# A diffusion trunk on one core: the experts' scatter through a sum of its own, and a finer spread of the modulation sums

## Chip, cores and metric

One core of one Trainium2 chip runs the whole kernel. The metric is the device time of one execution in microseconds, the median of several runs.

## What is computed

Two layers over 256 latent and 256 context tokens of width 1024, all in float32. Each layer modulates its input by vectors that come from a conditioning vector, mixes tokens (a recurrence, windowed attention, differential attention, one projection in and one out), adds and normalises; then a channel mixer, again modulated, gated and normalised. The channel mixer of layer 0 is a dense SwiGLU, that of layer 1 a top-2-of-8 mixture of SwiGLU experts over the latent tokens alone:

```
mod = split(silu(c) @ ada_w[layer] + ada_b[layer], 6)
u = h * (1 + mod[4]) + mod[3]
layer 0: f = (silu(u @ w1) * (u @ w3)) @ w2
layer 1: f = sum over e of combine[:, e] * swiglu(u, w1[e], w3[e], w2[e])
h = layer_norm(alpha * h + mod[5] * f, ln_g, ln_b)
```

The product with `mod[5]` is the same for all experts of a token row, column by column.

## The kernel before

Every weight is split into a high and a low part (`split`, L117 to L128): ScalarE copies a 128x1024 tile to `whi` (L126), VectorE subtracts it from the raw tile into `wlo` (L127), and TensorE makes three products of each pair (L107 to L109). The split tiles come from the pool `wp` with 5 buffers for each of the two parts, for all stages; the split of `w2` in the dense SwiGLU alone has another pool with 4. Raw weights come in tiles of 1 MB, issued in order from the SyncE queue.

**Dense SwiGLU** (`ffn`, L893 to L983). The hidden width of 2816 is worked in 11 steps of 256. `up(s)` loads and splits w1 and w3 of a step (two raw buffers, the pool `rawp`) and makes two parts, f = 0 and 1, of 48 products each, with SiLU and product on ScalarE and VectorE. `down(s)` makes 8 outputs of 6 products each in two PSUM banks (`ps_T`); VectorE copies (L956, step 0) or adds (L958) each into `acc`. The order is up(0); then for s = 0 to 8: up(s + 1), `fill(s)`, down(s); then up(10) and `last`. `fill` runs up to 4 pieces of another list, the modulation sums of layer 1 (`ada_vector`, L302 to L338). A piece loads 1 MB of `ada_w` into one of the same two raw buffers, and VectorE multiplies and adds it into `acca` (L319, L321): four operations where the vector is wanted for both kinds of tokens (vectors 0 and 1), two otherwise (vectors 2 to 5). After four such pieces the end of a vector transposes and reduces (L331, L332) and adds a bias (L337). There are 33 pieces in all, and one wait hangs on the first: `acca` lies where the layer norm's gains (`lg`, `lb`) lay, which GpSimd reads in `base` (L890).

**Mixture of experts** (`moe`, L1226 to L1309). Tokens are gathered into units of 128 for one expert; 7 units run, written out one behind another, and a loop for further ones runs no time with these inputs. A unit takes 33 raw tiles of 1 MB. `wtile` (L1066 to L1075) gives each a buffer in turn: 7 of the pool `rawb`, then 2 of `rawp`, so 9 tiles can be on the way or wait. `up` and `down` split and multiply them. At the end of a unit `scatter` (L1185 to L1200) splits its output Y, multiplies it with a selection matrix (two 128-row blocks by two halves of 512 columns, PSUM bank `ps_T`), and for each of the four results VectorE multiplies by the router's weight and by the gate row `mod[5]` into `sct` (L1199, two buffers), and GpSimd adds `sct` into the stream `hl` (L1200). In the last unit VectorE takes half of the adds.

The instructions of an engine stand in an order that is fixed when the program is built: a scheduler interleaves the parts by its own estimates, in the order of the source where it can. Each engine then works in that order.

Of the kernel before, what the change touches and what calls it, by code (L numbers as in the profile page):

```python
# [15 lines left out]
F32 = mybir.dt.float32  # L16
# [4 lines left out]
ALU = mybir.AluOpType  # L21
# [3 lines left out]
P = 128  # L25
D = 1024
KD = D // P
T = 512
# [8 lines left out]
UNITS = 7  # L37
# [39 lines left out]
class Trunk:  # L77
# [41 lines left out]
    def split(self, v, pool=None):  # L119

        nc = self.nc
        a, b = v.shape[1], v.shape[2]
        pool = pool or self.wp
# [260 lines left out]
    def fill(self, n):  # L384

        for _ in range(min(n, len(self.todo))):
            self.todo.pop(0)()
# [505 lines left out]
    def ffn(self, uh, ul, h, pools, gate, fill):  # L893
        nc, i = self.nc, self.i
        accp, raw2, wp2, gp = pools
# [6 lines left out]
        def up(s):  # L902
# [18 lines left out]
            for f in range(2):  # L921
                if s:
# [24 lines left out]
        def down(s, gs, gate):  # L947
            fs = [*zip(gs, w2_parts(s))]
            for tb in range(NTB):
                for n in range(2):  # L950
# [21 lines left out]
        for s in range(NS - 2):  # L972
            if s == NS - 4:
                with self.tc.issue_after(self.last.ins):
                    gate = gate()
            nxt = up(s + 1)
            fill(s)
            down(s, gs, gate)
            gs = nxt
        fs = [*zip(gs, w2_parts(NS - 2))]  # L980
        gs = up(NS - 1)
        fill(NS - 2)
# [202 lines left out]
    def scatter(self, Y, selT, cu, gate, hl, quick=False):  # L1185
# [6 lines left out]
        for b in range(2):  # L1192
            for nn in range(2):
                cs = slice(nn * 512, nn * 512 + 512)
                o = self.bank("h" if quick else "T")
                nc.tensor.matmul(o, lhsT=selT[:, b], rhs=yh[:, cs], start=True, stop=False)
                nc.tensor.matmul(o, lhsT=selT[:, b], rhs=yl[:, cs], start=False, stop=True)
                t = mp.tile([P, 512], F32, name="sct", tag="g" if quick and nn else "sct")
                nc.vector.scalar_tensor_tensor(out=t, in0=o, scalar=cu[:, b:b + 1], in1=gate[:, cs], op0=ALU.mult, op1=ALU.mult)  # L1199
                (nc.vector if quick and nn else nc.gpsimd).tensor_tensor(out=hl[:, b, cs], in0=hl[:, b, cs], in1=t, op=ALU.add)  # L1200
# [27 lines left out]
    def moe(self, hl, u, gate, ro, rs, pool, first):  # L1228
# [4 lines left out]
        gb = self.gains(1, 0, xr)  # L1233
        u32 = rp.tile([P, KD, 2 * P], F32, name="u32r")
# [34 lines left out]
        Y = None  # L1269
        for u in range(UNITS):  # L1270
# [20 lines left out]
            self.scatter(Y, selT, cu[:, :, u], gate, hl, u == UNITS - 1)  # L1291
# [3 lines left out]
        with tc.For_i(UNITS, n, 1) as u:  # L1295
# [12 lines left out]
            self.scatter(Y, selT, pc[:, 1], gate, hl)  # L1308
        return fin  # L1309

    def run(self):
# [5 lines left out]
        with ExitStack() as es:  # L1317
# [4 lines left out]
            self.wp = pool("wp", 5)  # L1322
# [35 lines left out]
            with tc.tile_pool(name="hc", bufs=1) as hcp:  # L1358
# [9 lines left out]
                with tc.tile_pool(name="acc", bufs=1) as accp, tc.tile_pool(name="raw2", bufs=1) as raw2, tc.tile_pool(name="wp2", bufs=4) as wp2, \  # L1368
# [5 lines left out]
                    with tc.tile_pool(name="ga", bufs=3) as gp:  # L1374
# [5 lines left out]
                        self.ffn(uh, ul, h, (accp, raw2, wp2, fg), lambda: self.gate(0, 5, [0, 1], gp, "x4"), lambda s: self.fill(4))  # L1380
# [23 lines left out]
            self.RB, self.wn = 7, 0  # L1404
            self.rawb = pool("rawb", self.RB)
            ro = pool("ro", 1)
# [56 lines left out]
```

## Time and profile before

| | us |
|---|---|
| runs, median (3 runs) | 1658.87 (1657.64 to 1660.73) |
| profiled execution, its own time | 1661.47 |
| profiled execution, its span | 1659.6 |
| TensorE busy (share of the span) | 1559.6 (94%) |
| VectorE busy | 1305.5 (79%) |
| ScalarE busy | 915.9 (55%) |
| GpSimd busy | 157.7 (10%) |

The rest of a time outside the span is 1.9 us. Times inside the trace count from the start of the span. The dense SwiGLU lies at about 318 to 717, the mixer of layer 1 at 717 to 880, the units of the experts at 929 to 1643. In the rows PE is TensorE, DVE VectorE, ACT ScalarE, POOL GpSimd, SP SyncE, whose queue issues the loads.

### The profile page before, as it was taken

How to read it: one execution, taken by the hardware profiler on the slowest of the kernel's cores; microseconds unless marked ns; L12 is line 12 of the kernel's file. 1: busy time of each engine (PE TensorE's matmuls, PEld its weight loads, DVE VectorE, ACT ScalarE, POOL GpSimd, SP SyncE). 2: the span in 40 equal slices, each digit the busy share in tenths (PEclk: the TensorE clock that was granted, in tenths of full speed). 3: DMA queues.
4: the chain of work that ended last, by engine and by line, in shares of the span. 5: the costliest groups of instructions: out<-in, count | busy, mean ns of one | idle time of the engine just before them, and what ended most of it. 6: DMA issues, size and time to landing. Idle time of an engine off the chain costs nothing. (4 is left out here: it accounts for less than half of the span.)

```text
span 1659.6 us, 21231 instructions
## 1 busy us (share of the span) xinstructions
PE 1559.6 (94%) x7753; PEld 1228.5 (74%) x7753; DVE 1305.5 (79%) x1835; ACT 915.9 (55%) x1292; POOL 157.7 (10%) x132
## 2 busy tenths in 40 slices
PE   7999999996999999989798799999999999999995
PEld 3776566785888887777576588787877878878774
DVE  2678674669977666677976999999888898888987
ACT  2466565422222222246765578777776767767673
POOL 0000011250000000250002200101000010010101
PEclk9999999997999999999799899999999999999998
DMA  9313446335556553112216599898998989989890
GB/s 306 122 57 102 153 153 203 101 129 162 207 188 196 185 183 122 52 60 77 76 26 254 211 394 352 333 360 309 350 353 310 335 322 342 356 306 339 326 351 31
DMA packets 167655, 364.78 MB, mean 220 GB/s; under 512 B 8396, under 2 KB 46120, under 8 KB 165496
## 3 DMA queue, kind: packets, MB, share of 16 engines
q1 hardware_dynamic: 162544, 355.56, 60.9%
q0 software_dynamic: 1840, 6.67, 1.2%
q10 hardware_dynamic: 3160, 1.12, 0.3%
q8 instruction: 64, 1.05, 0.2%
q14 instruction: 47, 0.39, 0.1%
HBM read 362.27 MB, written 1.05 MB: 219 GB/s over the span
## 5 line engine op out<-in xcount | busy, mean ns | idle before, releaser
L127 DVE TENSOR_TENSOR wlo<-rawb,whi 128x1024 fp32r<-128x1024 f32 x362 | 436.1, 1249 | 34.4 <-ACT whi L126 30.7
L126 ACT CAST whi<-rawb 128x1024 fp32r<-128x1024 f32 x362 | 364.3, 1051 | 56.8 <-PE ps_h L109 33.7
L126 ACT CAST whi<-raw 128x1024 fp32r<-128x1024 f32 x214 | 218.7, 1051 | 185.0 <-PE ps_T L109 86.1
L127 DVE TENSOR_TENSOR wlo<-raw,whi 128x1024 fp32r<-128x1024 f32 x214 | 268.7, 1283 | 46.2 <-ACT whi L126 44.7
L108 PE MATMUL ps_h<-wlo,th 128*128 128x512 f32 (+1 forms) x672 | 257.9, 384 | 14.2 <-DVE wlo L127 13.2
L107 PE MATMUL ps_h<-whi,th 128*128 128x512 f32 (+1 forms) x672 | 253.7, 378 | 0.2 <-ACT th L131 0.2
L109 PE MATMUL ps_h<-whi,tl 128*128 128x512 f32 (+1 forms) x672 | 251.7, 375 | 0.0
L108 PEld LDWEIGHTS ps_h<-wlo,th 128*128 128x128 f32 x672 | 127.3, 189 | 51.2 <-DVE wlo L127 30.5
L107 PEld LDWEIGHTS ps_h<-whi,th 128*128 128x128 f32 x672 | 127.2, 189 | 23.2 <-ACT th L131 0.5
L109 PEld LDWEIGHTS ps_h<-whi,tl 128*128 128x128 f32 x672 | 127.5, 190 | 20.7 <-DVE tl L132 0.3
L108 PE MATMUL ps_Y<-wlo,gTh 128*128 128x512 f32 x308 | 122.4, 397 | 0.4
L109 PE MATMUL ps_Y<-whi,gTl 128*128 128x512 f32 x308 | 120.3, 390 | 0.0
L1200 POOL TENSOR_TENSOR hl<-hl,sct 128x512 f32<-128x512 f32 x26 | 45.0, 1760 | 679.2 <-DVE sct L1199 679.2
L107 PE MATMUL ps_Y<-whi,gTh 128*128 128x512 f32 x308 | 108.3, 390 | 0.0
L107 PE MATMUL ps_acc<-uh,whi 128*128 128x512 f32 (+1 forms) x256 | 92.5, 367 | 2.3 <-ACT whi L126 2.3
L108 PE MATMUL ps_acc<-ul,whi 128*128 128x512 f32 (+1 forms) x256 | 94.3, 369 | 0.1
L109 PE MATMUL ps_acc<-uh,wlo 128*128 128x512 f32 (+1 forms) x256 | 92.2, 361 | 0.0
L108 PE MATMUL ps_S<-ul,whi 128*128 128x512 f32 (+1 forms) x240 | 85.6, 357 | 0.0
L107 PE MATMUL ps_S<-uh,whi 128*128 128x512 f32 (+1 forms) x240 | 85.5, 357 | 0.0
L109 PE MATMUL ps_S<-uh,wlo 128*128 128x512 f32 (+1 forms) x240 | 85.0, 355 | 0.0
L107 PE MATMUL ps_T<-whi,gh 128*128 128x512 f32 x152 | 61.5, 404 | 16.8 <-DVE acc L956 14.6
L321 DVE SCALAR_TENSOR_TENSOR acca<-raw,sc,acca 128x1024 f32<-128x1024 f32 x56 | 70.2, 1278 | 5.3 <-DMA raw<-in_ada_w_dram 5.1
(362 smaller groups left out, 2895.2 us busy)
## 6 DMA issues: line engine op xcount, KB each, us to landing
rawb<-in_moe_w_dram SPq DMA_DIRECT2D x181, 1024.0 KB, 6.5
raw<-in_moe_w_dram SPq DMA_DIRECT2D x50, 1024.0 KB, 6.6
raw<-in_ada_w_dram SPq DMA_DIRECT2D x40, 1024.0 KB, 5.1
raw<-in_ffn_w_dram SPq DMA_DIRECT2D x33, 1024.0 KB, 5.3
raw<-in_w_in_dram SPq DMA_DIRECT2D x16, 1024.0 KB, 5.1
aw<-in_ada_w_dram SPq DMA_DIRECT2D x16, 512.0 KB, 6.8
raw<-in_w_out_dram SPq DMA_DIRECT2D x16, 512.0 KB, 5.0
lg<-in_ln_g_dram POOLq DMA_DIRECT2D x4, 512.0 KB, 4.1
```

Of the source, the lines that this page charges most:

```text
L107: mm(out, lhsT=ah, rhs=bh, start=start, stop=False)
L108: mm(out, lhsT=ah, rhs=bl, start=False, stop=False)
L109: mm(out, lhsT=al, rhs=bh, start=False, stop=stop)
L126: nc.scalar.copy(out=hi, in_=v)
L127: self.last = nc.vector.tensor_tensor(out=lo, in0=v, in1=hi, op=ALU.subtract)
L321: STT(out=acc[t], in0=r[:, k - k0], scalar=x, in1=acc[t], op0=ALU.mult, op1=ALU.add)
L1200: (nc.vector if quick and nn else nc.gpsimd).tensor_tensor(out=hl[:, b, cs], in0=hl[:, b, cs], in1=t, op=ALU.add)
```

## The change

- `scatter` hands each of its four results to a function. For units 0 to 5 it is `add_sum`: VectorE multiplies by the router's weight and adds into a sum tile of 128x2048, in one operation (unit 0 multiplies only). GpSimd has no part in it.
- After unit 5 `fold` runs on GpSimd: two products of the sum with the gate row and two adds into `hl`, each 128x1024. Unit 6 goes as before (`add_last`).
- The split tiles of the experts and of what is split just ahead of them take a sixth pair of buffers (`wpx`), in turn with the five. The raw tiles of the experts have 5 buffers in place of 7, so 7 with the two of `rawp`. A small tile `shift` moves the addresses behind it.
- In `ffn` the pieces of the modulation sums no longer stand four together between up(s + 1) and down(s). From s = 1 on one stands ahead of each of the two parts of up(s + 1), and one ahead of the second and the fourth row block of down(s). Step 0 has none. What is left (one piece of 33) runs ahead of `last`.

```
--- before.py
+++ after.py
@@ -120,7 +120,9 @@
 
         nc = self.nc
         a, b = v.shape[1], v.shape[2]
-        pool = pool or self.wp
+        if pool is None:
+            pool = self.wps[self.ws % len(self.wps)]
+            self.ws += 1
         hi = pool.tile([P, 1024], F32R, name="whi", tag="whi")[:, 0:a * b].rearrange("p (a b) -> p a b", a=a)
         lo = pool.tile([P, 1024], F32R, name="wlo", tag="wlo")[:, 0:a * b].rearrange("p (a b) -> p a b", a=a)
         nc.scalar.copy(out=hi, in_=v)
@@ -899,7 +901,7 @@
         acc = accp.tile([P, NTB, D], F32, name="acc")
         NS = FF // 256
 
-        def up(s):
+        def up(s, fill=None):
             ws = []
             for w in (w1, w3):
                 r = self.raw(w[:, :, s * 256:(s + 1) * 256])
@@ -919,6 +921,8 @@
                         for f in range(2):
                             product(bs[f][j], ws[j], f, t0, t1)
             for f in range(2):
+                if fill:
+                    fill(1)
                 if s:
                     b1, b3 = self.bank("acc"), self.bank("S")
                     product(b1, ws[0], f, 0, T)
@@ -944,9 +948,11 @@
             for j, ((gh, gl), (wh, wl)) in enumerate(fs):
                 self.mm3(b, gh[:, t], gl[:, t], wh[:, 0, cs], wl[:, 0, cs], j == 0, j == len(fs) - 1)
 
-        def down(s, gs, gate):
+        def down(s, gs, gate, fill):
             fs = [*zip(gs, w2_parts(s))]
             for tb in range(NTB):
+                if fill and tb % 2:
+                    fill(1)
                 for n in range(2):
                     cs = slice(n * 512, n * 512 + 512)
                     b = self.bank("T")
@@ -973,13 +979,12 @@
             if s == NS - 4:
                 with self.tc.issue_after(self.last.ins):
                     gate = gate()
-            nxt = up(s + 1)
-            fill(s)
-            down(s, gs, gate)
+            nxt = up(s + 1, fill if s else None)
+            down(s, gs, gate, fill if s else None)
             gs = nxt
         fs = [*zip(gs, w2_parts(NS - 2))]
         gs = up(NS - 1)
-        fill(NS - 2)
+        fill(99)
         last(fs + [*zip(gs, w2_parts(NS - 1))], gate)
 
 
@@ -1182,7 +1187,7 @@
             self.split2(th[:, ks], tl[:, ks], pt.rearrange("p (k t) -> p k t", k=4))
         return th, tl
 
-    def scatter(self, Y, selT, cu, gate, hl, quick=False):
+    def scatter(self, Y, selT, cu, add):
 
         nc, mp = self.nc, self.mp
         yh, yl = (mp.tile([P, D], F32R, name=name, tag="rows") for name in ("yh", "yl"))
@@ -1192,12 +1197,39 @@
         for b in range(2):
             for nn in range(2):
                 cs = slice(nn * 512, nn * 512 + 512)
-                o = self.bank("h" if quick else "T")
+                o = self.bank("h" if add is self.add_last else "T")
                 nc.tensor.matmul(o, lhsT=selT[:, b], rhs=yh[:, cs], start=True, stop=False)
                 nc.tensor.matmul(o, lhsT=selT[:, b], rhs=yl[:, cs], start=False, stop=True)
-                t = mp.tile([P, 512], F32, name="sct", tag="g" if quick and nn else "sct")
-                nc.vector.scalar_tensor_tensor(out=t, in0=o, scalar=cu[:, b:b + 1], in1=gate[:, cs], op0=ALU.mult, op1=ALU.mult)
-                (nc.vector if quick and nn else nc.gpsimd).tensor_tensor(out=hl[:, b, cs], in0=hl[:, b, cs], in1=t, op=ALU.add)
+                add(b, nn, o, cu[:, b:b + 1])
+
+    def add_sum(self, b, nn, o, cu):
+
+        S = self.sum[:, b, nn * 512:nn * 512 + 512]
+        if (b, nn) in self.summed:
+            self.nc.vector.scalar_tensor_tensor(out=S, in0=o, scalar=cu, in1=S, op0=ALU.mult, op1=ALU.add)
+        else:
+            self.nc.vector.tensor_scalar(S, o, cu, None, ALU.mult)
+        self.summed.add((b, nn))
+
+    def add_last(self, b, nn, o, cu):
+
+        cs = slice(nn * 512, nn * 512 + 512)
+        t = self.mp.tile([P, 512], F32, name="sct", tag="g" if nn else "sct")
+        self.nc.vector.scalar_tensor_tensor(out=t, in0=o, scalar=cu, in1=self.gate2[:, cs], op0=ALU.mult, op1=ALU.mult)
+        (self.nc.vector if nn else self.nc.gpsimd).tensor_tensor(out=self.hl[:, b, cs], in0=self.hl[:, b, cs], in1=t, op=ALU.add)
+
...
+    def fold(self):
+
+        for op in (ALU.mult, ALU.add):
+            for b in range(2):
+                S = self.sum[:, b]
+                self.nc.gpsimd.tensor_tensor(out=S if op == ALU.mult else self.hl[:, b], in0=S, in1=self.gate2 if op == ALU.mult else self.hl[:, b], op=op)
 
     def moe_consts(self, ro):
 
@@ -1231,6 +1263,8 @@
         xr, rp = pool("xr", 1, "right"), rs.enter_context(tc.tile_pool(name="rq", bufs=1))
         xh, xl = xr.tile([P, 2, D], F32R, name="xh"), xr.tile([P, 2, D], F32R, name="xl")
         gb = self.gains(1, 0, xr)
+        self.sum, self.summed, self.hl, self.gate2 = xr.tile([P, 2, D], F32, name="sum"), set(), hl, gate
+        self.add_last = self.add_last
         u32 = rp.tile([P, KD, 2 * P], F32, name="u32r")
         lt, logit = rp.tile([P, 2, P], F32, name="lt"), ro.tile([P, 2, NE], F32, name="logit")
         lg, lp = self.bank("T"), self.bank("T")
@@ -1288,7 +1322,9 @@
                     Y = [self.bank("Y") for _ in range(2)]
                 self.down(e, c, gt, Y)
                 g = nxt
-            self.scatter(Y, selT, cu[:, :, u], gate, hl, u == UNITS - 1)
+            self.scatter(Y, selT, cu[:, :, u], self.add_last if u == UNITS - 1 else self.add_sum)
+            if u == UNITS - 2:
+                self.fold()
             if u + 1 < UNITS:
                 x, selT = x2, selT2
         n = nc.values_load(nu[0:1, 0:1], min_val=0, max_val=NU)
...
@@ -1319,7 +1355,7 @@
             self.cp = pool("cp", 1)
             self.stp = pool("stp", 4)
             self.rawp = pool("rawp", 2)
-            self.wp = pool("wp", 5)
+            self.wps, self.ws = [pool("wp", 5)] * 5, 0
             pool("edge", 1, side="right").tile([P, 24], F32, name="edge")
             mx = ExitStack()
             right = lambda name, bufs, **kw: mx.enter_context(tc.tile_pool(name=name, bufs=bufs, side="right", **kw))
@@ -1377,7 +1413,7 @@
                         self.todo = sum((self.ada_vector(1, c, [0, 1], gp, rw) for c in range(2)), [])
                         self.todo += [lambda: m1.extend(self.mods(1, 0, (0, 1)))]
                         self.todo += sum((self.ada_vector(1, c, [0], gp, rw) for c in range(2, 6)), [])
-                        self.ffn(uh, ul, h, (accp, raw2, wp2, fg), lambda: self.gate(0, 5, [0, 1], gp, "x4"), lambda s: self.fill(4))
+                        self.ffn(uh, ul, h, (accp, raw2, wp2, fg), lambda: self.gate(0, 5, [0, 1], gp, "x4"), self.fill)
                         self.fill(99)
 
                 self.rest = "res"
@@ -1401,8 +1437,10 @@
             self.moe_consts(pool("rc", 1))
             mh, ml = self.mixer(1, uh, ul, lat, bd, self.lru_products(1, uh, ul, True), prepare)
             self.dumpm(mh, ml, 1)
-            self.RB, self.wn = 7, 0
+            self.RB, self.wn = 5, 0
             self.rawb = pool("rawb", self.RB)
+            pool("shift", 1).tile([P, 32], F32, name="shift")
+            self.wps, self.ws = self.wps + [pool("wpx", 1)], 0
             ro = pool("ro", 1)
             gate2 = self.gate(1, 5, [0], ro)[0]
             with ExitStack() as ms:
```

## Rows read from the trace of the kernel before

**Rows 1.** Busy tenths of TensorE, 40 equal slices of the span.

```profile
PE   7999999996999999989798799999999999999995
```

**Rows 2.** Engines by stretch: busy us (count) per engine, granted clock, DMA share, GB/s.

```profile
360.00:380.00 20.00, 12.51 (x56) 10.02 (x54) 15.36 (x16) 1.12 (x2) 3.93 (x2) 0.89 0.32 106
380.00:400.00 20.00, 12.87 (x45) 10.32 (x46) 17.36 (x22) 5.55 (x7) 0.00 (x0) 0.68 0.57 176
420.00:440.00 20.00, 19.91 (x91) 16.19 (x90) 19.53 (x30) 4.28 (x5) 0.00 (x0) 1.00 0.47 168
...
1240.00:1260.00 20.00, 17.20 (x69) 13.16 (x68) 18.41 (x18) 12.46 (x14) 7.02 (x4) 0.91 0.75 266
```

**Rows 3.** Timeline of TensorE, dense SwiGLU, step 0: start, us, instruction, [idle before, releaser].

```profile
387.13 0.79 PE L107 MATMUL ps_T<-whi,gh 128*128 128x512 f32 x1 [14.62 <-DVE acc L956]
...
388.14 0.63 PE L109 MATMUL ps_T<-whi,gl 128*128 128x512 f32 x1
```

**Rows 4.** Timeline of VectorE in the same stretch.

```profile
363.96 1.42 DVE L319 TENSOR_SCALAR acca<-raw,sc 128x1024 f32<-128x1024 f32 x2 [8.75 <-POOL hl L890]
...
365.90 7.26 DVE L321 SCALAR_TENSOR_TENSOR acca<-raw,sc,acca 128x1024 f32<-128x1024 f32 x6
...
386.40 0.67 DVE L956 COPY acc<-ps_T 128x512 f32<-128x512 f32 x1
```

**Rows 5.** Costliest groups: busy, mean ns | idle before, releaser.

```profile
L321 DVE SCALAR_TENSOR_TENSOR acca<-raw,sc,acca 128x1024 f32<-128x1024 f32 x56 | 70.2, 1278 | 5.3 <-DMA raw<-in_ada_w_dram 5.1
```

**Rows 6.** Timeline of VectorE in step 1 of the dense SwiGLU.

```profile
431.09 0.69 DVE L958 TENSOR_TENSOR acc<-ps_T,acc 128x512 f32<-128x512 f32 x1 [0.23 <-PE ps_T L109]
```

**Rows 7.** Timeline of VectorE in step 8 of the dense SwiGLU.

```profile
643.62 0.69 DVE L930 TENSOR_TENSOR silu<-silu,ps_S 128x512 f32<-128x512 f32 x1 [7.08 <-PE ps_S L109]
```

**Rows 8.** Waits of TensorE, 940 to 1640: us in total, times, longest.

```profile
PE ps_h L108 <- DVE wlo L127: 13.2, 15, 1.2
```

**Rows 9.** Timeline of GpSimd in the experts: second, fourth and sixth scatter.

```profile
1139.73 1.30 POOL L1200 TENSOR_TENSOR hl<-hl,sct 128x512 f32<-128x512 f32 x1 [91.74 <-DVE sct L1199]
...
1346.28 7.01 POOL L1200 TENSOR_TENSOR hl<-hl,sct 128x512 f32<-128x512 f32 x4 [97.70 <-DVE sct L1199]
...
1554.49 1.30 POOL L1200 TENSOR_TENSOR hl<-hl,sct 128x512 f32<-128x512 f32 x1 [97.65 <-DVE sct L1199]
```

**Rows 10.** Timeline of VectorE at the fourth scatter.

```profile
1346.81 1.86 DVE L127 TENSOR_TENSOR wlo<-rawb,whi 128x1024 fp32r<-128x1024 f32 x1
...
1349.85 0.75 DVE L1199 SCALAR_TENSOR_TENSOR sct<-ps_T,cu,gate 128x512 f32<-128x512 f32 x1 [0.52 <-POOL hl L1200]
1350.52 3.86 DVE L127 TENSOR_TENSOR wlo<-rawb,whi 128x1024 fp32r<-128x1024 f32 x2
...
1354.90 5.75 DVE L127 TENSOR_TENSOR wlo<-rawb,whi 128x1024 fp32r<-128x1024 f32 x5
```

**Rows 11.** Timeline of TensorE at the fourth scatter.

```profile
1348.72 0.50 PE L108 MATMUL ps_h<-wlo,th 128*128 128x512 f32 x1 [0.84 <-DVE wlo L127]
...
1352.20 0.50 PE L108 MATMUL ps_h<-wlo,th 128*128 128x512 f32 x1 [1.15 <-DVE wlo L127]
...
1354.43 0.49 PE L108 MATMUL ps_h<-wlo,th 128*128 128x512 f32 x1 [0.79 <-DVE wlo L127]
```

**Rows 12.** Timeline of GpSimd in `base`, ahead of the dense SwiGLU's step 0.

```profile
353.49 5.74 POOL L890 TENSOR_TENSOR hl<-hl,lg 128x1024 f32<-128x1024 f32 x2
359.19 4.74 POOL L890 TENSOR_TENSOR hl<-hl,lb 128x1024 f32<-128x1024 f32 x2
```

**Rows 13.** Timeline of VectorE beside it.

```profile
351.19 3.42 DVE L127 TENSOR_TENSOR wlo<-raw,whi 128x1024 fp32r<-128x1024 f32 x1
```

**Rows 14.** Loads: count, KB each, median us from issue to landing.

```profile
rawb<-in_moe_w_dram SPq DMA_DIRECT2D x181, 1024.0 KB, 6.5
```

**Rows 15.** Waits of ScalarE, 940 to 1640: first and last of nine rows.

```profile
ACT g L1109 <- PE ps_h L109: 48.7, 37, 3.0
...
ACT whi L126 <- DVE sct L1199: 0.3, 1, 0.3
```

More of the change, by code (lines that the diff above doesn't have):

```diff
@@ L921, in up @@
             for f in range(2):
+                if fill:
+                    fill(1)
                 if s:
@@ L945, in products, with down @@
                 self.mm3(b, gh[:, t], gl[:, t], wh[:, 0, cs], wl[:, 0, cs], j == 0, j == len(fs) - 1)
-        def down(s, gs, gate):
+        def down(s, gs, gate, fill):
             fs = [*zip(gs, w2_parts(s))]
             for tb in range(NTB):
+                if fill and tb % 2:
+                    fill(1)
                 for n in range(2):
@@ L975, in ffn @@
                     gate = gate()
-            nxt = up(s + 1)
-            fill(s)
-            down(s, gs, gate)
+            nxt = up(s + 1, fill if s else None)
+            down(s, gs, gate, fill if s else None)
             gs = nxt
@@ L1183, in turn, with scatter @@
         return th, tl
-    def scatter(self, Y, selT, cu, gate, hl, quick=False):
+    def scatter(self, Y, selT, cu, add):
         nc, mp = self.nc, self.mp
@@ L1194, in scatter, with add_sum, add_last, add_one @@
                 cs = slice(nn * 512, nn * 512 + 512)
-                o = self.bank("h" if quick else "T")
+                o = self.bank("h" if add is self.add_last else "T")
                 nc.tensor.matmul(o, lhsT=selT[:, b], rhs=yh[:, cs], start=True, stop=False)
                 nc.tensor.matmul(o, lhsT=selT[:, b], rhs=yl[:, cs], start=False, stop=True)
-                t = mp.tile([P, 512], F32, name="sct", tag="g" if quick and nn else "sct")
-                nc.vector.scalar_tensor_tensor(out=t, in0=o, scalar=cu[:, b:b + 1], in1=gate[:, cs], op0=ALU.mult, op1=ALU.mult)
-                (nc.vector if quick and nn else nc.gpsimd).tensor_tensor(out=hl[:, b, cs], in0=hl[:, b, cs], in1=t, op=ALU.add)
+                add(b, nn, o, cu[:, b:b + 1])
+    def add_sum(self, b, nn, o, cu):
+        S = self.sum[:, b, nn * 512:nn * 512 + 512]
+        if (b, nn) in self.summed:
+            self.nc.vector.scalar_tensor_tensor(out=S, in0=o, scalar=cu, in1=S, op0=ALU.mult, op1=ALU.add)
+        else:
+            self.nc.vector.tensor_scalar(S, o, cu, None, ALU.mult)
+        self.summed.add((b, nn))
+    def add_last(self, b, nn, o, cu):
+        cs = slice(nn * 512, nn * 512 + 512)
+        t = self.mp.tile([P, 512], F32, name="sct", tag="g" if nn else "sct")
+        self.nc.vector.scalar_tensor_tensor(out=t, in0=o, scalar=cu, in1=self.gate2[:, cs], op0=ALU.mult, op1=ALU.mult)
+        (self.nc.vector if nn else self.nc.gpsimd).tensor_tensor(out=self.hl[:, b, cs], in0=self.hl[:, b, cs], in1=t, op=ALU.add)
+    def add_one(self, b, nn, o, cu):
+        cs = slice(nn * 512, nn * 512 + 512)
+        t = self.mp.tile([P, 512], F32, name="sct", tag="sct")
+        self.nc.vector.scalar_tensor_tensor(out=t, in0=o, scalar=cu, in1=self.gate2[:, cs], op0=ALU.mult, op1=ALU.mult)
+        self.nc.gpsimd.tensor_tensor(out=self.hl[:, b, cs], in0=self.hl[:, b, cs], in1=t, op=ALU.add)
+    def fold(self):
+        for op in (ALU.mult, ALU.add):
+            for b in range(2):
+                S = self.sum[:, b]
+                self.nc.gpsimd.tensor_tensor(out=S if op == ALU.mult else self.hl[:, b], in0=S, in1=self.gate2 if op == ALU.mult else self.hl[:, b], op=op)
     def moe_consts(self, ro):
@@ L1233, in moe @@
         gb = self.gains(1, 0, xr)
+        self.sum, self.summed, self.hl, self.gate2 = xr.tile([P, 2, D], F32, name="sum"), set(), hl, gate
+        self.add_last = self.add_last
         u32 = rp.tile([P, KD, 2 * P], F32, name="u32r")
@@ L1290, in moe @@
                 g = nxt
-            self.scatter(Y, selT, cu[:, :, u], gate, hl, u == UNITS - 1)
+            self.scatter(Y, selT, cu[:, :, u], self.add_last if u == UNITS - 1 else self.add_sum)
+            if u == UNITS - 2:
+                self.fold()
             if u + 1 < UNITS:
@@ L1307, in moe @@
                 g = nxt
-            self.scatter(Y, selT, pc[:, 1], gate, hl)
+            self.scatter(Y, selT, pc[:, 1], self.add_one)
         return fin
```

16 lines of the change are left out of this document (10 added, 6 removed).

## The prediction

> **What bounds the kernel now.** I read the busy tenths first: TensorE is at 9 in most slices from the dense SwiGLU on [rows 1], so a change pays only where it fills a hole of that engine, and the holes are the thing to look for. The view by stretch finds two kinds. In the dense SwiGLU a full 20 us hold 91 matmuls, but the two stretches from 360 to 400 hold 56 and 45, at a granted clock of 0.89 and 0.68 [rows 2]. In the experts the stretches with a scatter are short in the same way: 69 matmuls at 1240 to 1260, with 7.02 us of GpSimd beside them [rows 2].
>
> The first hole is one wait: TensorE stood 14.62 us for VectorE's copy out of the bank `ps_T` [rows 3], and then ran some ten matmuls 0.42 us apart (387.72 to 388.14) instead of 20/91 = 0.22, the lower of the clock's two levels, 1.2 GHz [rows 2, 3]. VectorE's timeline says why: it waited 8.75 us for GpSimd's `base`, since the first sum lies where `base` reads its gains, and then worked off the step's four pieces of the modulation sums, 16 operations from 363.96 on (the first rows of them stand), before it came to the copy at 386.40 [rows 4]. The data were there; the fixed order put the copy behind them.
>
> The second kind is told by the waits: TensorE waited 13.2 us in 15 waits for `wlo`, VectorE's half of the split [rows 8]. At the fourth scatter there are three of them, 0.84 + 1.15 + 0.79 = 2.78 us [rows 11], so five scatters like it and a lighter first one make up the row. Around them VectorE's splits grow: 5.75/5 = 1.15 us each where GpSimd is idle, but 1.86 and 3.86/2 = 1.93 beside GpSimd's adds, and one multiply waits 0.52 us for a buffer that GpSimd holds [rows 10]. The multiply itself, which reads PSUM and one tile of SBUF, is no longer for it (0.75) [rows 10]. Loads bound nothing here: of ScalarE's nine rows of waits none names a DMA [rows 15].
>
> **Part 1: the dense SwiGLU.** Step 0 gets no pieces. Its wait on `base` and the 20 us of sums leave VectorE's queue there, and the copies L956 come when their bank is full. The price of the hole is the matmuls missing: 91 + 91 - 56 - 45 = 81, times 20/91, is 17.8 us. What is late next? The raw buffers that the pieces held go to the weights of up(2) instead, earlier than before, and their splits are held by TensorE's own use of the split tiles, so I see no new wait in step 0. But the work is not gone. Pieces 0 to 3 now fall into step 1: 16 operations of 1.28 us [rows 5], 20.4 us. VectorE's other work in a step is 4 + 2 splits of 1.2, 8 adds of 0.69 [rows 6] and about 3 us of SiLU, 15.5 in all, and a step has 144 matmuls, 144 x 20/91 = 31.7 us. So step 1 asks VectorE for 36 us, steps 2 and 3 (two pieces with four operations, two ends) for about 32. The stretch of before that is like it, 420 to 440, has VectorE busy 19.53 of 20 and TensorE 19.91 [rows 2]; there the adds wait for TensorE, not TensorE for them (0.23 us) [rows 6]. So full use was borne at no cost; the 36 - 31.7 = 4.3 us over in step 1 is partly carried on. I take 3 us, between 0 and 8 (4.3 and as much again from a bad order).
>
> At the other end the list runs one step longer: pieces 28 to 31, 8 operations, 10.2 us, fall into step 8, where `down` also has the residual. VectorE waited 7.08 us for TensorE in that step [rows 7], which covers most; I take 1 us, 0 to 3. The loads move with the pieces on SyncE's queue: they stand one by one between a step's weight loads instead of in one block ahead of w2's. A step still issues at most seven, and what stands behind them is due a step later, so I cost this at 0; if that cover were gone, it would be the landing of one load, some 6.5 us [rows 14], where it first runs short. Part 1: -17.8 + 3 + 1 = **-13.8 us** (-18 to -5).
>
> **Part 2: the scatter without GpSimd, and a sixth pair of split tiles.** Of a scatter's VectorE work the operation stays (multiply and add from PSUM for multiply by two from PSUM: same engine, same 128x512 form, so 0; even a fifth of 0.75 more on 24 operations would be 3.6 us of VectorE, of which TensorE would see a part). Removed are 24 adds on GpSimd. VectorE gets back 0.71 (1.86 - 1.15) + 1.56 (3.86 - 2.30) + 0.52 = 2.8 us at each scatter [rows 10], as much as TensorE waits there (2.78) [rows 11]. The sixth pair lets the splits run one more tile ahead, 6 matmuls or 1.3 us. So at units 0 to 4 the waits should go. What they cost in all is read from the period of the scatters: GpSimd's start is its own 7.02 plus its idle time after the last one, 91.74 + 7.02 = 98.8 us for the first period, 97.65 + 7.02 = 104.7 for the last [rows 9]. From the first scatter to the sixth, 1554.49 - (1139.73 - 98.76) = 513.5 us went for five periods; five of 98.8 would be 494. So 19.5 us is the most. The least is the waits alone, 13.2 - 2.8 = 10.4 us. The rest between is the slow clock behind a stop (0.91 at 1240 [rows 2]) and small waits; I take half of it, **-15 us** (-19.5 to -10).
>
> **Part 3: the fold.** Behind unit 5 GpSimd runs four operations of 128x1024. The nearest rows are those of `base`: two adds take 4.74 us with VectorE quiet, 2.37 each, and 5.74 where a split fell among them [rows 12]; a split of VectorE beside them took 3.42 us instead of 1.15 [rows 13]. That is 1.15 + 2.3: it stands for a whole operation of GpSimd. So four operations can hold four splits by 2.27 each, 9.1 us. The 2.8 us that GpSimd costs at this scatter today go, which leaves 6.3; the sixth pair takes 1.3 off: **+5 us** on TensorE. Bounds: +8 with the slow clock behind a long stop; -3 if the four fall beside operations of VectorE that read PSUM, which are not held [rows 10]. Nobody else waits: `hl` is not read until unit 6's scatter, some 88 us later. The Trainium skill, GPSIMD Engine Reference, section Engine selection, gives element-wise work to VectorE, as GpSimd is about half as fast at two inputs; rows 12 and 10 agree (2.37 against 1.15). By that rule the fold would be better as four operations of VectorE, 4.6 us by the same rows, which is no less than what I charge for it here, so the sum stays.
>
> **Part 4: seven raw tiles instead of nine.** A unit of 98.8 us takes 33 tiles, 3.0 us each. Nine in turn give a tile 27 us from one release to the next use of its place, seven 21. A load needs 6.5 [rows 14] and the two splits with their wait for room some 5, so about 9 us are left where there were 15. I cost it at 0 in the units, and at 0.5 (0 to 3) at the start, where two tiles fewer are ready. If the cover were gone, each landing would be waited for.
>
> **Sum.** -13.8 - 15 + 5 + 0.5 = -23.3. The profiled execution's own time was 1661.5, so 1638.2; the median of the runs lies 2.6 us lower, so **1636 us** (rounded). The bounds of the parts, added with some offset, reach from 1624 to 1648.
>
> **Rivals.** (a) *The stop moves to step 1.* The order is fixed by estimates, and it has put 16 operations ahead of the copies once. If pieces 0 to 3 stand ahead of down(1)'s adds, most of part 1 is lost: 1636 + 12 = 1648. For it: step 1 is overfull on VectorE. Against: in the steps behind the first the adds were never late [rows 6]. (b) *Adds queue behind a load.* A piece ahead of the second and fourth row blocks of down(s) stands in VectorE's order; if its 1 MB has not landed, the adds wait, and with them TensorE, which has only two banks, 12 matmuls or 2.6 us. Twelve of the 16 such places are loads, the others ends. At a whole landing each that is 12 x (6.5 - 2.6) = 47 us, 1636 + 47 = 1683. It decides from 23/12, some 2 us per place; at 3 us it gives 1636 + 36 = 1672, slower than before. Against: in all 56 operations VectorE waited 5.3 us for these loads [rows 5]. (c) *Seven tiles starve the splits.* The unit would then go at the rate of loads: at 3.1 us a tile instead of 3.0, 7 x 33 x 0.1 = 23 us, which gives 1659, no change. Against: 9 us of room. (d) *The fold costs nothing and all of the 19.5 goes*: 1636 - 4.5 - 8 = 1623. (e) *The scatters don't get faster*, since another operation than GpSimd's holds the splits: 1636 + 15 = 1651. Against: rows 10 are plain.
>
> **How the numbers follow.** Forecast 0.60 (1628 to 1645), (a) 0.14, (b) 0.06, (c) 0.06, (d) 0.07, (e) 0.07. A measurement of this kernel tells about 0.2%, 3.3 us, from no change. The forecast, (a), (d) and (e) are faster, 0.88, less 0.01 for the ends of (a) and (e); that 0.01 and (c) are the same, 0.07; (b) is slower, 0.06. The range, to hold 8 in 10, leaves out (b), (c) and the ends of (d): 1622 to 1652.
>
> **What would show it.** Right: no wait of TensorE on L956 near 380, and matmuls of about 90 per 20 us there; no operation of GpSimd between two scatters of the experts, splits at 1.15 to 1.2 us beside them and periods near 99 us; at the end of unit 5 four operations of GpSimd of 2.4 to 3.4 us, splits of 3.4 beside them, and one stop of TensorE of some 8 us in all. Wrong: waits on L958 in step 1 (a), VectorE waiting for `ada_w` ahead of an add (b), ScalarE waiting for `moe_w` (c).

## The result and the profile after

| | before | after |
|---|---|---|
| median of 4 runs each, side by side (us) | 1658.26 (1654.81 to 1660.73) | 1636.57 (1635.87 to 1637.11) |
| profiled execution: its time, its span | 1661.47, 1659.6 | 1635.87, 1634.0 |

The ratio is 0.9872, with an interval of 0.9854 to 0.989: faster by 1.3%. The forecast was 1636. The median fell by 21.7 us, the span of the profiled executions by 25.6. This is how the 25.6 divide (but for rounding), by the starts of instructions that both traces have:

| stretch (first instruction to first instruction) | before | after | difference |
|---|---|---|---|
| start to `base` (GpSimd's first product with `lg`) | 353.5 | 351.9 | -1.5 |
| `base` to layer 1's mixer (TensorE's first product with `hl`) | 365.1 | 350.5 | -14.6 |
| mixer and router, to the first expert product | 211.1 | 209.6 | -1.5 |
| first expert product to the first scatter (first `yl`) | 109.0 | 108.0 | -1.0 |
| first period, scatter to scatter | 98.2 | 99.6 | +1.4 |
| second to fifth period together | 415.3 | 402.9 | -12.4 |
| last period, with the fold after | 88.2 | 91.9 | +3.7 |
| behind it, to the end of the span | 19.2 | 19.6 | +0.4 |

The first and the third row, 3.0 us, hold nothing that the change is meant to speed up. In the runs below the start to `base` varies between 351.9 and 356.3 and the third row between 208.7 and 211.1, so these rows are read as the scatter of single executions; without them the span fell by 22.6, near the 21.7 of the medians.

The columns of all views are those of the rows of before. After, TensorE is busy for 6.5 us less and GpSimd for 26 us less:

```profile
PE 1553.1 (95%) x7753; PEld 1221.8 (75%) x7753; DVE 1300.9 (80%) x1835; ACT 909.2 (56%) x1292; POOL 131.4 (8%) x112
```

Engines by stretch, after: the hole of the dense SwiGLU, step 1, the third scatter, the fold.

```profile
360.00:380.00 20.00, 18.61 (x83) 15.06 (x82) 16.34 (x16) 4.76 (x6) 4.30 (x2) 1.00 0.42 134
380.00:400.00 20.00, 20.00 (x90) 16.58 (x89) 19.86 (x22) 5.83 (x7) 0.00 (x0) 1.00 0.54 176
420.00:440.00 20.00, 20.00 (x91) 16.58 (x90) 16.09 (x20) 6.96 (x9) 0.00 (x0) 1.00 0.74 242
1220.00:1240.00 20.00, 19.68 (x86) 15.29 (x85) 19.85 (x22) 16.29 (x19) 0.00 (x0) 1.00 0.88 313
1520.00:1540.00 20.00, 16.04 (x55) 10.92 (x55) 19.82 (x16) 11.78 (x14) 13.09 (x4) 0.83 0.68 233
```

The first hole is nearly filled: 83 and 90 matmuls where [rows 2] had 56 and 45, at a granted clock of 1.00 (2.4 GHz). The stretch with a scatter holds 86 and nothing of GpSimd. The last line is the new hole: 55 matmuls beside 13.09 us of GpSimd.

VectorE in step 0 and 1, after, where [rows 4, 6] are of before. The first copy comes at 374.33, twelve us earlier, between two operations of a piece, and an add of step 1 waits for TensorE as it did. The pieces have not left step 0: in the fixed order 3 of their first 16 operations stand ahead of the first copy, where before had all 16, and the other 13 follow between it and the first add of step 1.

```profile
370.60 1.42 DVE L321 TENSOR_SCALAR acca<-raw,sc 128x1024 f32<-128x1024 f32 x2 [1.60 <-DMA raw<-in_ada_w_dram]
...
372.53 1.28 DVE L323 SCALAR_TENSOR_TENSOR acca<-raw,sc,acca 128x1024 f32<-128x1024 f32 x1
...
374.33 1.28 DVE L962 COPY acc<-ps_T 128x512 f32<-128x512 f32 x2
375.53 1.27 DVE L323 SCALAR_TENSOR_TENSOR acca<-raw,sc,acca 128x1024 f32<-128x1024 f32 x1
...
408.32 0.69 DVE L964 TENSOR_TENSOR acc<-ps_T,acc 128x512 f32<-128x512 f32 x1 [0.23 <-PE ps_T L109]
```

Waits of TensorE in the whole dense SwiGLU (345 to 660), after: 2.9 us for `acc`, where one of them alone was 14.62 [rows 3]. The 1.4 is a wait for the first copy, and VectorE worked without a stop from the 1.60 us of its own wait for `ada_w`, shown above, to that copy.

```profile
PE ps_T L107 <- DVE acc L964: 1.5, 3, 1.0
PE ps_T L107 <- DVE acc L962: 1.4, 1, 1.4
```

VectorE in the experts, after: the starts of five scatters (`yl`), and the third of them whole.

```profile
1020.01 1.28 DVE L134 TENSOR_TENSOR yl<-ps_Y,yh 128x512 fp32r<-128x512 f32 x2
...
1119.59 1.28 DVE L134 TENSOR_TENSOR yl<-ps_Y,yh 128x512 fp32r<-128x512 f32 x2
...
1220.33 1.28 DVE L134 TENSOR_TENSOR yl<-ps_Y,yh 128x512 fp32r<-128x512 f32 x2
1221.77 1.44 DVE L1209 SCALAR_TENSOR_TENSOR sum<-ps_T,cu,sum 128x512 f32<-128x512 f32 x2 [0.15 <-PE ps_T L1202]
1223.13 1.22 DVE L129 TENSOR_TENSOR wlo<-raw,whi 128x1024 fp32r<-128x1024 f32 x1
1224.26 1.40 DVE L1209 SCALAR_TENSOR_TENSOR sum<-ps_T,cu,sum 128x512 f32<-128x512 f32 x2
...
1522.44 0.69 DVE L134 TENSOR_TENSOR yl<-ps_Y,yh 128x512 fp32r<-128x512 f32 x1
...
1614.38 1.29 DVE L134 TENSOR_TENSOR yl<-ps_Y,yh 128x512 fp32r<-128x512 f32 x2 [2.19 <-ACT yh L133]
```

The split between the scatter's operations takes 1.22, where it took 1.86 and 1.93 beside GpSimd [rows 10], and an operation of the scatter takes 0.75, as the old one did (the two at 1221.77 overlap a little, 1.44 together). The periods are 99.6 (1119.59 - 1020.01), then 100.7, three more of (1522.44 - 1220.33)/3 = 100.7, and 91.9.

Whole periods by engine: the fourth and the fifth of before, and the third of after.

```profile
1343.91:1447.46 103.55, 100.46 (x470) 81.00 (x469) 90.98 (x90) 73.44 (x85) 7.01 (x4) 1.00 0.93 334
1447.46:1552.16 104.70, 101.65 (x470) 82.25 (x469) 90.78 (x89) 73.46 (x85) 7.02 (x4) 0.98 0.92 331
```

```profile
1220.33:1321.04 100.71, 100.15 (x470) 81.02 (x469) 88.75 (x91) 72.82 (x85) 0.00 (x0) 1.00 0.97 344
```

The fourth of before holds the three waits of [rows 11], 2.78 us, and 103.55 - 2.78 = 100.8, within 0.1 us of the period after, in which no wait of TensorE is listed. The fifth has waits of the same size and 1.15 us more beside a granted clock of 0.98.

GpSimd, VectorE and TensorE at the fold, after, one timeline each.

```profile
1525.43 3.30 POOL L1232 TENSOR_TENSOR sum<-sum,gate 128x1024 f32<-128x1024 f32 x1 [623.26 <-DVE sum L1209]
1528.81 3.25 POOL L1232 TENSOR_TENSOR hl<-sum,hl 128x1024 f32<-128x1024 f32 x1
1532.02 3.36 POOL L1232 TENSOR_TENSOR sum<-sum,gate 128x1024 f32<-128x1024 f32 x1
1535.45 3.22 POOL L1232 TENSOR_TENSOR hl<-sum,hl 128x1024 f32<-128x1024 f32 x1
```

```profile
1525.26 1.22 DVE L129 TENSOR_TENSOR wlo<-rawb,whi 128x1024 fp32r<-128x1024 f32 x1
...
1527.71 2.10 DVE L129 TENSOR_TENSOR wlo<-rawb,whi 128x1024 fp32r<-128x1024 f32 x1
1529.74 3.40 DVE L129 TENSOR_TENSOR wlo<-rawb,whi 128x1024 fp32r<-128x1024 f32 x1
...
1533.66 2.79 DVE L129 TENSOR_TENSOR wlo<-rawb,whi 128x1024 fp32r<-128x1024 f32 x1
1536.38 3.38 DVE L129 TENSOR_TENSOR wlo<-rawb,whi 128x1024 fp32r<-128x1024 f32 x1
```

```profile
1529.87 0.50 PE L108 MATMUL ps_h<-wlo,th 128*128 128x512 f32 x1 [1.02 <-DVE wlo L129]
...
1533.19 0.79 PE L108 MATMUL ps_h<-wlo,th 128*128 128x512 f32 x1 [1.90 <-DVE wlo L129]
```

Four splits take 2.10, 3.40, 2.79 and 3.38 us where an undisturbed one takes 1.22: the fold held them by 0.9, 2.2, 1.6 and 2.2, 6.8 us in all. Each ends 1.1 us after one of GpSimd's four operations (1525.43 + 3.30 = 1528.73, and 1527.71 + 2.10 = 1529.81), so it ran about its own length once that operation was over. TensorE waits four times, and these four are all its waits for `wlo` in the units (940 to 1640), where [rows 8] had 15:

```profile
PE ps_h L108 <- DVE wlo L129: 3.7, 4, 1.9
```

### The profile page after: what moved, and what is told of

The parts are those of the page before. It is cut to its first block, busy times and chain, and to the rows that moved or that the text cites. A ratio compares the mean times of both kernels' runs of the same rounds, so it can differ in the third digit from the quotient of the medians.

```text
span 1634.0 us, 21131 instructions
## 1 busy us (share of the span) xinstructions
PE 1553.1 (95%) x7753; PEld 1221.8 (75%) x7753; DVE 1300.9 (80%) x1835; ACT 909.2 (56%) x1292; POOL 131.4 (8%) x112
## 5 line engine op out<-in xcount | busy, mean ns | idle before, releaser
L129 DVE TENSOR_TENSOR wlo<-rawb,whi 128x1024 fp32r<-128x1024 f32 x330 | 393.0, 1238 | 28.4 <-ACT whi L128 27.1
L129 DVE TENSOR_TENSOR wlo<-raw,whi 128x1024 fp32r<-128x1024 f32 x246 | 306.6, 1276 | 60.0 <-ACT whi L128 59.1
L128 ACT CAST whi<-raw 128x1024 fp32r<-128x1024 f32 x246 | 249.7, 1051 | 185.3 <-PE ps_T L109 85.7
L128 ACT CAST whi<-rawb 128x1024 fp32r<-128x1024 f32 x330 | 328.7, 1051 | 32.7 <-PE ps_h L109 15.0
L107 PE MATMUL ps_S<-uh,whi 128*128 128x512 f32 (+1 forms) x240 | 85.4, 357 | 0.0
L108 PE MATMUL ps_acc<-wlo,uh 128*128 128x512 f32 (+1 forms) x176 | 69.2, 393 | 1.8 <-DVE wlo L129 1.8
L107 PE MATMUL ps_acc<-whi,uh 128*128 128x512 f32 (+1 forms) x176 | 70.9, 403 | 0.0
```

The lines of the kernel that those rows point to most:

```text
L107: mm(out, lhsT=ah, rhs=bh, start=start, stop=False)
L108: mm(out, lhsT=ah, rhs=bl, start=False, stop=False)
```

## The experiments

The kernel before ran beside each group of experiments, and the ratios are to it. Its median was 1655.31 beside the first four, 1658.6 beside the next four (old scatter, no fold, fold on VectorE, fold spread) and 1655.54 beside the last four. Medians of different groups are not set against one another to a microsecond; for that the marks of the table above are used. With the new scatter the steady period repeats within some 0.3 us (100.6 to 100.9); with the old one it is about 103.5 or 104.7.

**The dense SwiGLU alone.** The kernel before with the part of the diff that concerns `ffn`.

> The kernel before with the change of the dense SwiGLU alone: step 0 without pieces of the modulation sums, then one piece at a time. The experts are as before. Theory: the hole at 372 to 387 goes and nothing else moves, 16 us less (in the changed kernel layer 1's first products came 16.2 us earlier): about 1642. Rival: the new order of the rest of the program was part of it, and alone it gives under 10 us.

Measured: 1642.61, ratio 0.9926 (0.9904 to 0.9949). From `base` to the mixer 350.8 us against 365.1: -14.3. The periods are 98.2, 102.3, three times 103.5, and 88.2: those of before, but for its two of 104.7. So 2.4 us of the -12.4 in the table above also go where nothing of the experts is changed; why the granted clock was 0.98 in those two and not in these isn't shown.

**The same pieces in blocks of four, from step 1.** This is meant to tell the empty step 0 from the finer spread.

```
-            fill(s)
+            if s:
+                fill(s)
...
         fill(NS - 2)
+        fill(NS - 2)
```

> The kernel before, in which step 0 has no pieces and all later steps have them in one block of four between up and down, as before. Theory A: the empty step 0 is the whole gain; time as with the pieces one at a time, about 1642, no wait on the copy out of ps_T in step 0. Rival B: the spread matters too; then TensorE waits for an add in step 1, where 20.4 us of sums stand in one block, by some 5 to 15 us: 1647 to 1657.

Measured: 1641.5, ratio 0.991 (0.989 to 0.9929), and 349.8 us from `base` to the mixer. By stretch, as above, this kernel:

```profile
360.00:380.00 20.00, 18.60 (x82) 15.08 (x81) 16.16 (x17) 4.90 (x6) 5.56 (x2) 1.00 0.37 111
380.00:400.00 20.00, 20.00 (x90) 16.54 (x89) 19.89 (x21) 5.36 (x7) 0.00 (x0) 1.00 0.53 179
```

VectorE, this kernel:

```profile
371.86 1.42 DVE L319 TENSOR_SCALAR acca<-raw,sc 128x1024 f32<-128x1024 f32 x2 [1.61 <-DMA raw<-in_ada_w_dram]
...
375.59 1.28 DVE L956 COPY acc<-ps_T 128x512 f32<-128x512 f32 x2
```

82 and 90 matmuls, as with the spread. So the gain of part 1 is that the pieces no longer stand in a body ahead of step 0's copies; writing them one at a time brought nothing that can be measured. But VectorE's order is nearly the same in both kernels: here too 3 operations stand ahead of the first copy and 13 between it and the first add of step 1, since the scheduler takes the block apart. What a block kept whole would cost was not tested.

**The experts alone.** The changed kernel with the old order in `ffn` (`up(s + 1)`, four pieces, `down(s)`).

> The changed kernel with the dense SwiGLU of before: blocks of four, from step 0. Theory: the experts' part gives what its trace shows, the periods of the scatters 100.7 us in place of up to 104.7, the last unit 3.7 us longer: some 8 us less than before, about 1650. Rival: the two parts help each other and this alone gives under 4 us.

Measured: 1650.25, ratio 0.9958 (0.9933 to 0.9982); periods 99.6, then 100.6 to 100.7, and 91.9 as in the changed kernel. The two halves add up within the intervals: 0.9926 x 0.9958 = 0.9884, and both together gave 0.9872.

**Without the sixth pair.** Its place goes back to raw tiles, eight in turn.

```
-            self.RB, self.wn = 5, 0
+            self.RB, self.wn = 6, 0
...
-            self.wps, self.ws = self.wps + [pool("wpx", 1)], 0
```

> The changed kernel without the sixth pair of split tiles; its room goes to one raw tile more (6 in place of 5). Theory: the sum without GpSimd is what shortens the scatter, and the sixth pair is worth its 1.3 us of lead at each of seven scatters at most: 0 to 8 us slower than the changed kernel, 1637 to 1645, periods of 100.7 to 102. Rival: the pair carries the gain; periods go back to 103 to 104.7 and the time to about 1650.

Measured: 1636.59, ratio 0.989 (0.9866 to 0.9913), span 1633.4. The periods are 98.3, then 100.7 four times, then 91.9. TensorE's waits for `wlo` in the units:

```profile
PE ps_h L108 <- DVE wlo L129: 5.0, 4, 1.9
```

So the pair takes 1.3 us off the waits at the fold (5.0 to 3.7), just the six matmuls that the prediction gave it, but the last period is 91.9 with and without it, and the steady one 100.7. It buys no time that can be measured.

**The old scatter under the rest of the change.** The function `add_one` does what the scatter did before: VectorE multiplies into `sct`, GpSimd adds into `hl`. There is no fold; the sixth pair and the seven raw tiles stay.

```
-            self.scatter(Y, selT, cu[:, :, u], self.add_last if u == UNITS - 1 else self.add_sum)
-            if u == UNITS - 2:
-                self.fold()
+            self.scatter(Y, selT, cu[:, :, u], self.add_last if u == UNITS - 1 else self.add_one)
```

> The changed kernel with the scatter of before in units 0 to 5 (multiply by weight and gate, add on GpSimd, no sum, no fold); the sixth pair and the five raw tiles stay. Theory: GpSimd's adds hold VectorE's splits, whatever the number of pairs; periods of the scatters go back to 102 to 104 and the last unit to 88 (no fold): about 1642, as with the change of the dense SwiGLU alone (1642.6). Rival: the sixth pair absorbs the hold; periods of 100.7 and, without a fold, about 1633.

Measured: 1647.14 (two runs), ratio 0.9935 (0.991 to 0.9959). The first period is 100.8, the later ones are 103.5 to 104.8 again, the last 88.2, and the waits for `wlo` are back:

```profile
PE ps_h L108 <- DVE wlo L129: 14.7, 16, 1.2
```

So GpSimd's adds are what made the periods long, and six pairs don't help against them. By its ratio this kernel is where the dense SwiGLU's change alone is (0.9926).

**No fold.** The four operations are left out, and with them the experts' sum of units 0 to 5 never reaches `hl`.

> The changed kernel without the fold: the sum of units 0 to 5 is not multiplied by the gate row and not added to the stream, so the output lacks these units. Theory: the last unit (first product stretch to its scatter) goes from 91.9 to some 84 us, as the stop of 7.8 us behind the sixth scatter was the fold's: about 1629. Rival: half of that stop is the scatter's own burst, as before; then 88 us and about 1633.

Measured: 1629.95, ratio 0.9833 (0.9816 to 0.9849). The last period is 85.4 in place of 91.9: the fold costs 6.5 us. The stretch of the fold, this kernel:

```profile
1520.00:1540.00 20.00, 19.59 (x84) 14.80 (x83) 19.86 (x22) 15.49 (x18) 0.00 (x0) 1.00 0.90 307
```

84 matmuls against 55 make 29 x 20/91 = 6.4 us, nearly the same from another view. Of it 3.7 are waits. The rest stands beside a granted clock of 0.83 instead of 1.00: in the changed kernel the matmuls behind the longest wait come 0.43 us apart, where those ahead of it came 0.24 apart.

```profile
1530.20 0.40 PE L109 MATMUL ps_h<-whi,tl 128*128 128x512 f32 x1
1530.44 0.40 PE L107 MATMUL ps_h<-whi,th 128*128 128x512 f32 x1
...
1534.21 0.63 PE L107 MATMUL ps_h<-whi,th 128*128 128x512 f32 x1
1534.64 0.63 PE L108 MATMUL ps_h<-wlo,th 128*128 128x512 f32 x1
```

**The fold on VectorE.**

```
-                self.nc.gpsimd.tensor_tensor(out=S if op == ALU.mult ...
+                self.nc.vector.tensor_tensor(out=S if op == ALU.mult ...
```

> The changed kernel with the fold on VectorE: four operations of 128x1024 with two inputs from SBUF. Theory: by the splits' rows they take 1.15 to 1.2 us each, 4.7 in all, against the 7 to 9 us by which GpSimd's hold the splits; the last unit gets shorter by 2 to 4 us: 1633 to 1635. Rival: TensorE loses the same, as VectorE is what it waits for in both: 1636.5.

Measured: 1636.24, ratio 0.9866 (0.985 to 0.9883); last period 91.4 against 91.9. VectorE, this kernel:

```profile
1529.59 2.35 DVE L1232 TENSOR_TENSOR sum<-sum,gate 128x1024 f32<-128x1024 f32 x2
1531.86 2.35 DVE L1232 TENSOR_TENSOR hl<-sum,hl 128x1024 f32<-128x1024 f32 x2
1534.13 1.22 DVE L129 TENSOR_TENSOR wlo<-rawb,whi 128x1024 fp32r<-128x1024 f32 x1
```

The four operations take 1.18 us each instead of 3.3. But they stand together ahead of the splits, 4.7 us, and TensorE waits 3.3 us for `whi` and 0.9 for `wlo`, with 58 matmuls at 0.86 in that stretch. The Trainium skill, GPSIMD Engine Reference, section Engine selection, gives element-wise work to VectorE; it holds for the operation (1.18 against 2.37 with VectorE quiet [rows 12], 3.3 beside the splits), and the kernel gains nothing that can be measured. TensorE's order is another one here (it takes a product of `ps_Y` where it took one of `ps_h`), and why it waits for ScalarE's `whi` isn't shown.

**The fold spread over the last unit.** One operation of GpSimd behind each of the first four parts of unit 6; a tiny operation of VectorE ahead of each (one column of `sum`, plus zero times a column of a tile of that part) makes it wait for its turn.

```
...
+                if u == UNITS - 1 and c < 4:
+                    self.fold_step(c, nxt)
...
```

> The changed kernel with the four operations of the fold apart: one each on GpSimd behind chunks 0 to 3 of the last unit, each held until that chunk's g is there by a one-column operation of VectorE on the sum. Theory: a held split costs some 2.3 us each time and VectorE has under 2 us to spare in a chunk and one to two tiles of lead, so TensorE loses 0.5 to 1 us a time in place of 2: last unit 87 to 89, about 1633. Rival: the hold costs the same wherever it stands: no change, 1636.5.

Measured: 1637.07, ratio 0.987 (0.9854 to 0.9886); last period 92.2. GpSimd, this kernel:

```profile
1544.44 8.98 POOL L1232 TENSOR_TENSOR sum<-sum,gate 128x1024 f32<-128x1024 f32 x1 [637.20 <-DVE sum L1230]
...
1560.15 3.31 POOL L1232 TENSOR_TENSOR sum<-sum,gate 128x1024 f32<-128x1024 f32 x1 [6.73 <-DVE sum L1230]
```

VectorE beside these two:

```profile
1544.27 4.62 DVE L129 TENSOR_TENSOR wlo<-raw,whi 128x1024 fp32r<-128x1024 f32 x4
1548.81 2.35 DVE L129 TENSOR_TENSOR wlo<-rawb,whi 128x1024 fp32r<-128x1024 f32 x2
...
1559.98 4.56 DVE L129 TENSOR_TENSOR wlo<-rawb,whi 128x1024 fp32r<-128x1024 f32 x2
```

The expectation fell. The first operation came while six splits ran back to back at their usual 1.15 to 1.18; it took 8.98 us and no split was held: it ended 2.3 us after the last of the six (1553.42 and 1551.16), about its length alone. The second held one split by 2.2 us (4.56 for two), and so did the last two; TensorE waited 5.0 us in three waits. A split is due every 1.5 us (66 in 100.7), and three held splits at three places cost about what four at one place cost. Here the granted clock was 1.00 over the whole last period, and it was still 6.8 us longer than without a fold (92.2 and 85.4); so beside the 5.0 of waits some 1.8 are left that the clock does not explain.

**Five raw tiles in turn** (the pool `rawb` with 3 in place of 5).

> The changed kernel with 3 raw tiles of the experts' own, so 5 in turn with the two others, in place of 7. Theory of the prediction: seven leave some 9 us of room over a load's 6.5 and the splits' 5; five give a turn of 5 x 3.05 = 15 us, room of 3.5, just enough: 0 to 10 us slower, first waits of ScalarE on loads, 1637 to 1647. Rival: the loads were already near their rate, and each tile less costs; then periods of 105 and more, over 1660.

Measured: 1639.12, ratio 0.9898 (0.9874 to 0.9921). To the first scatter 110.3, first period 100.6, the later ones 100.6. ScalarE waits for loads, which it doesn't in the changed kernel:

```profile
ACT whi L128 <- DMA rawb<-in_moe_w_dram: 4.2, 5, 1.0
ACT whi L128 <- DMA raw<-in_moe_w_dram: 3.8, 5, 1.1
```

8.0 us of waits, and the marks differ only at the start: (110.3 + 100.6) - (108.0 + 99.6) = 3.3 us. So the rate of the units is not that of the loads, even with five.

**Without the tile `shift`**, which no instruction uses.

> The changed kernel without the small tile that moves the addresses behind it by 128 bytes. Theory: addresses do not matter, 1636.5, splits at 1.22 us. Rival: they do; the splits of the sixth pair or the routing's tiles get slower and with them the periods.

Measured: 1639.77, ratio 0.9905 (0.9882 to 0.9929), span 1636.3. The periods are 100.9 instead of 100.7 and the last is 92.7; the span is 2.3 us longer. In the steady periods no large kind of instruction (over 100 of them) differs in duration by more than 0.4%. The two intervals overlap, so an effect of the tile isn't shown.

**The gate at the end.** Unit 6 goes into the sum as well; then the gate and the addition to `hl`, half on VectorE and half on GpSimd, once behind everything. No fold.

```
...
+        self.nc.vector.scalar_tensor_tensor(out=S, in0=o, scalar=cu, in1=S, op0=ALU.mult, op1=ALU.add)
+        eng.tensor_tensor(out=S, in0=S, in1=self.gate2[:, cs], op=ALU.mult)
+        eng.tensor_tensor(out=self.hl[:, b, cs], in0=self.hl[:, b, cs], in1=S, op=ALU.add)
...
```

> The changed kernel with unit 6 added into the sum too and the gate and the stream applied once behind it, half on VectorE and half on GpSimd; no fold. Theory: the last unit is 85.4 us as without a fold (6.5 less), and the end behind it grows by four to eight operations of 128x512, 2 to 4 us: 1632 to 1634, a version better than both. Rival: GpSimd and VectorE hold each other at the end, where nothing is beside them, and the whole 6.5 us comes back: 1636.5.

Measured: 1634.04, ratio 0.9876 (0.9849 to 0.9902), span 1630.4. The last period is 85.3 where it was 91.9, and what stands behind it 22.5 us (in the changed kernel 19.6): -6.6 + 2.9 = -3.7. TensorE has no wait for `wlo` left in the units. So by the trace it is the better version; the intervals of the two ratios overlap, and the times alone don't show it.

**Two scatters fewer.** Units 2 and 3 are not scattered, so their outputs are missing in the sum. This asks what a scatter still costs once GpSimd has no part in it.

> The changed kernel, in which units 2 and 3 are not scattered: no split of their output, no selection product, no sum, so the output lacks them. It asks what keeps the periods at 100.7 us where 98.8 was forecast. Theory: the burst of the scatter (six operations of VectorE, 4.1 us, and 8 matmuls, 1.8 us); without it the units next to it take under 97. Rival: VectorE is short of time all through the unit, and the unit takes its 100.7 less the 8 matmuls, 98.9.

Measured: 1629.74 (one run). The second scatter and the fifth, this kernel, VectorE:

```profile
1119.72 1.28 DVE L134 TENSOR_TENSOR yl<-ps_Y,yh 128x512 fp32r<-128x512 f32 x2
...
1415.68 1.28 DVE L134 TENSOR_TENSOR yl<-ps_Y,yh 128x512 fp32r<-128x512 f32 x2
```

Three periods took 296.0 us, in the changed kernel 302.1: 3.05 us for each scatter left out. Its eight matmuls are 8 x 20/91 = 1.8 of them. The other 1.3 may belong to the scatter's burst on VectorE (two `yl` and four operations, 1.28 + 1.44 + 1.40 = 4.1 us), but no wait of TensorE is listed there, so that isn't shown. A unit without a scatter is then 100.7 - 3.05 = 97.65, between the two values expected (under 97, and 98.9).

## Why the prediction was right

**Part 1, -13.8 predicted, -14.6 measured.** The wait on the copy fell from 14.62 to 1.4 us, and alone the part gave -14.3. By the starts on VectorE, 10.5 us lie ahead of the first copy and 4.2 between it and the first add of step 1. The hole was a little smaller than counted: 83 and 90 matmuls came, not 91 and 91, so 72 x 20/91 = 15.8 where the step had 17.8. What was charged against it was also smaller, and here the account in the prediction was off: pieces 0 to 3 did not fall into step 1 but ran between step 0's copies and the first add of step 1 (13 of 16 operations), so step 1 was not overfull. It took 34.7 us from its first add to that of step 2, three more than 144 matmuls at full rate, but before's step 1 took 35.7, so it was no new cost; steps 2 to 7 cost 0.3 and the end 0.8. Rival (a) is out: TensorE waited for the adds of step 1 and later for 1.5 us in all. Rival (b) happened once and small, and in step 0, where the prediction saw no new wait: VectorE's 1.60 us for `ada_w` stood ahead of the first copy, and TensorE waited 1.4 us for that copy.

**Part 2, -15 predicted, -12.0 measured** (-1.0 + 1.4 - 12.4). That GpSimd's adds hold the splits was right: the splits beside the scatter are at 1.22, and the old scatter brought the long periods back, so rival (e) is out. The step that was off is the floor: the first period of before (98.8 by GpSimd's rows, 98.2 by `yl`) was taken as what all units would fall to. It is a short one: with nine or eight raw tiles it is 98.2 and 98.3, with seven 99.6, with five 100.6, while the steady period is 100.7 with five, seven and eight alike, and the scatter itself is 3.05 of it. With the right floor the five periods could fall by 19.5 - 4 x (100.7 - 98.8) = 11.9 at most, where the step had 19.5 and took 15; they fell by 11.0. The floor stood in the trace of before: the fourth period less its waits, 100.8. What went are the waits, the step's least (10.4), and 2.4 us of the two periods of 104.7, which also went in the run with the dense SwiGLU alone; against them the first period grew by some 2 us, its wait of 0.6 left out. The 13.2 us of waits are also made up otherwise than the prediction read them: 0.6 at the first scatter, 1.4 at the second and 2.8 at each of the next four. The sixth pair's share was wrong as well: its six matmuls show in the waits and not in the time.

**Part 3, +5 predicted, +3.7 measured** (91.9 - 88.2). The mechanism held: the longest splits are 3.40 and 3.38, where 3.42 was forecast. The fold's own cost is 6.5, in place of the 2.8 of the old scatter; the step had 9.1, less 1.3 for the sixth pair, less 2.8. Measured are 6.8 us of held splits, four of them but only two by the full 2.2, and nothing off for the pair. The prediction put the 4.6 us of a fold on VectorE at no less than its own 5; by these figures it is a little less, and measured the two are alike (last periods of 91.4 and 91.9). Rival (d), a fold at no cost, is out.

**Part 4, 0.5 predicted, 0.4 measured:** start and first period together are 207.6 us with seven tiles and six pairs, and 207.2 with eight and five; it lies within the -12.0. Rival (c) is out: even five tiles cost 3.3 us, and at the start alone.

The parts made -23.3 together, and the stretches that they touch gave -14.6 - 12.0 + 3.7 = -22.9. They missed by -0.8, +2.5 (parts 2 and 4) and -1.3: the time came closer than the steps did, since they missed in both directions. That the forecast lies within 1 us of the median is in this part luck.

## What to carry to other kernels

Ahead of costing an edit, look at what stands between a full PSUM bank and its copy in the fixed order of the evacuating engine: here moving one step's filler work from that place was the whole gain of the dense SwiGLU's part, and a finer spread in the source, which the scheduler had made anyway, gave none. A steady rate is to be read from the middle of a loop, less the waits that the change is to remove (103.55 - 2.8 here), since a first period can be short for what was stocked up at the start. The fold cost about the same on GpSimd, on VectorE, or in four places; by the trace it got cheaper only at the end of the kernel, where no split is left to hold.

## What the runs showed of the hardware

- Who comes first goes on, and the other stands until it is done: an operation of GpSimd with two inputs of 128x1024 that came in ahead of a split held it by 2.2 us (in the spread fold it ended at 1563.46, the split at 1564.54), while one that met six splits back to back was itself stretched from 2.37 [rows 12] to 8.98 us, ended 2.3 us after the last of them and held none. The time that the profile gives for either therefore has the wait in it. The Trainium skill, GPSIMD Engine Reference, section Specifications, says that GpSimd shares its SBUF interfaces with VectorE and contends with its operations of two SBUF inputs; both rows agree, and a scatter's operation of VectorE that reads PSUM and one SBUF tile took 0.75 us with GpSimd idle and 0.75 beside it [rows 10].
- A stop of a few short waits drew more than its length: 3.7 us of waits at the fold went with a loss of 6.5, while the granted clock fell to 0.83 in that stretch; with the fold left out it was 1.00. In the spread fold the clock stayed at 1.00, and 5.0 us of waits went with a loss of 6.8.
